# A third gate pair as block products, linear-attention scores masked by a multiply, and another order of the last transposes

## The chip, the cores and the metric

The kernel runs on one core of a Trainium2 chip, in one launch. The metric is the device time of that launch in microseconds, as the median of several runs. The engines are TensorE (PE, whose weight loads are listed apart as PEld), VectorE (DVE), ScalarE (ACT), GpSimd (POOL) and SyncE (SP), which here only issues transfers; POOL issues some too. The profile of one execution gives times from the first instruction on.

## The reference

One layer of a streaming encoder runs on 512 prompt tokens and 64 sample tokens, each with its own state:

```python
x = x + mixer(rmsnorm(x))         # gated DeltaNet branch and gated linear attention (GLA) branch
x = x + cross_attn(rmsnorm(x))    # 4 heads into 256 memory tokens
x = x + conv_ffn(rmsnorm(x))      # up, causal conv of width 3, silu gate, down
y = rmsnorm(x)
# in the mixer:
proj = h @ w_in                   # q k v b a z_a | q_b k_b v_b g_lr z_b | gt_a gt_b
o_a = rmsnorm(gated_delta(conv_silu(q, k, v), g, beta, s_a)) * silu(z_a)
o_b = rmsnorm(gla(q_b, k_b, v_b, log_a, s_b)) * silu(z_b)
merged = sigmoid(gt_a) * (o_a @ w_out_a) + sigmoid(gt_b) * (o_b @ w_out_b)
return merged @ w_o
# in gla, per chunk of 64 tokens:
a_qk = where(tri, (q * exp(G)) @ (k * exp(-G)).T, 0)
```

`x` has 1024 features. All is float32. The outputs are `y` for both streams, the new states of both recurrences and of the two convolutions, and the memory keys and values.

## The kernel before

**Layout.** Features lie on the 128 partitions in eight blocks, the 576 tokens on the free axis: 512 of the prompt, then 64 of the sample. A float32 product is made of three: weights and activations are split into a high part in a reduced format and the rest (`xh`, `xl` for the normed input, `ach`, `acl` for block sums of two operands), and high by high, high by rest and rest by high are added up in PSUM. PSUM holds four tiles called `bank` and four called `sm`.

**Plain output tiles.** A tile of 128 output features is 8 feature blocks x 3 terms x 2 column halves (256 and 320), 48 matmuls into two banks. Another engine then evacuates the two banks, and the next tile but one uses them again. The evacuation of `q`, `k`, `v` heads goes to `u` and then through the causal convolution (`c`, `th`), that of the GLA inputs to `qb`, `kb`.

**Pairs as seven products.** A pair of tiles can be made as seven products of block sums, in the manner of Winograd's variant of Strassen (P1, P2, P3 and Q4 to Q7): the 576 columns are two halves of 288, the eight feature blocks pair up to four operands, and each product has 4 x 3 = 12 matmuls of 288 columns, 84 in all. `product_order` gives their order. The weight block sums are `ws`, `sums` of raw tiles `wr`; results are added into the gate tiles `gt` (`gate_finish`). Gate tiles come in pairs (`gta`, `gtb`) for m = 0 to 7; those from `GPLAIN` on are made as products, so three pairs are plain and five products. Their activation operands, `xops`, come from a chain `c_x`, which loads `x` again (`y`) and is started in front of the tile that `XAT` names.

**Weights.** SP loads raw tiles `wr` (three buffers, `RAWB`, and one more after the pools are swapped). They become high and rest tiles `w` (six buffers, three more after the swap). In `split_summed` ACT writes minus the raw tile and its rounded form, and POOL issues a transfer that adds the raw values from memory: `w<-wt`, or `w<-ws` for a block sum. Elsewhere ACT rounds and DVE or POOL subtracts. At pair m = 5 (`GSWAP`) the buffers of the recurrences are released and their space goes to a new pool (`swap_pools`).

**What sets the order.** The order of PE is made at build time. Chains of small work, written as generators (recurrences `c_gdn`, `c_gla`, statistics `c_rstat`, gates, splits), are put between the projection matmuls where a planner thinks their inputs ready. It keeps planned times for each engine from fixed costs, places each DVE, ACT, POOL and transfer instruction at the first free planned time behind its inputs, and issues all in order of planned time. So a small edit changes the order on every engine around it, and each engine's queue runs strictly in that order. Every instruction is recorded through one helper, so that in the profile all rows have line 288.

**Statistics.** For a norm, squares of the eight blocks are added up on DVE and POOL (`acc`, `sq`), then `ssq` sums over partitions with matmuls of one column, one for each 128 tokens and each tile given to it. At the end `roots` does this with `acc` and the squares of tiles 6 and 7 (`sqt`), and POOL takes the power.

**The end.** The last block of FFN makes output tiles 6 and 7 in two column parts each, `half(m, lo, hi)`. `flip(t, i, qs)` transposes blocks of token tile t, `roots` makes its scales, `out(t)` scales (half on ACT, half on DVE) and SP stores 512 KB. Token tiles 0 and 1 need the last half; tile 4 is the sample's 64 tokens, stored in two parts `yo`.

Of the kernel before, what the change touches and what calls it, by code (L numbers as in the profile page):

```python
# [12 lines left out]
I32 = mybir.dt.int32  # L13
# [13 lines left out]
HT = T // 2  # L27
NS = 57
RAWB = 3
# [80 lines left out]
MPAIRS = [(("mo", m), ("mo", m + 1)) for m in range(2, 8, 2)]  # L110
GPLAIN = 3
GSPLIT = 6
GSWAP = 5
XAT = ("zb", 2)
GPAIRS = [(("gta", m), ("gtb", m)) for m in range(GPLAIN, 8)]
# [360 lines left out]
def tile_trunk(ctx, tc, xT, memT, wt, wd, vec, cst, w0, wgate, st_gdn, st_conv, st_gla, st_ffn, ckT, cv,  # L476
# [26 lines left out]

    def tiny(w, s="t", bufs=8):
# [419 lines left out]
    def evac(ps, t_, gap=False, o1=0, o2=TP):  # L924
        for o, i, r in zip(two(t_, gap, o1, o2), pv(ps, gap), two(N["rbc"], gap)):
            V.tensor_tensor(o, i, r, op=ALU.mult)

# [92 lines left out]
    def c_gdn(h):  # L1020
# [176 lines left out]
        if h == 4:  # L1197
# [23 lines left out]
            for i in range(4):  # L1221
                S2 = small("S", 6)
                V.scalar_tensor_tensor(S2, sgd[:, i, :], dl[:, 16 + i:17 + i], pc[:, 128 * i:128 * i + 128], op0=ALU.mult, op1=ALU.add)
                DMO(o_gdn_s[i], S2)
            yield
        S = None
        for i in range(4 if h < 4 else 0):
            ci = 4 * i + h
            if S is not None:
                pc = sm()  # L1230
                PE.matmul(pc[0:n, 0:128], ks_[i], S, start=True, stop=True)
                R = small("R", 4)[0:n, :]
# [6 lines left out]
            vn = small("vn", 4)  # L1239
# [9 lines left out]
            S2 = small("S", 6)  # L1249
# [24 lines left out]
    def c_gla(p):  # L1274
# [9 lines left out]

        def pairs(s):

            out, full = [], []
            for i in range(3):
                t_ = slot(s)
                w_ = 512 if i < 2 else 256  # L1290
                G.memset(t_[:, 0:w_], 0.0)
                yield [t_]
                v_ = t_[:, 0:w_].rearrange("p (t a b) -> p t a b", a=2, b=128)
                out += [v_[:, k] for k in range(w_ // 256)]
                full.append(v_)
            return out, full

        aqb, _ = yield from pairs("aqb")
        kgt, kgt2 = yield from pairs("kgt")
        qgp = [slot(f"qgp{j}")[:, 0:T] for j in range(2)]  # L1300
# [24 lines left out]
        for t in range(5):  # L1325
            n = 128 if t < 4 else 64
            pa = sm()
            for j in range(2):
                PE.matmul(pa[0:n, 128 * j:128 * j + n], kx[:, 128 * t:128 * t + n], qgp[j][:, 128 * t:128 * t + n], start=True, stop=True)
            V.copy_predicated(aqb[t][0:n, :, 0:n], glam[0:n, 0:n].bitcast(I32).unsqueeze(1).broadcast_to([n, 2, n]),  # L1330
                              r4(pa[0:n, 0:256])[:, :, 0:n])
            yield
        vt = []
        for j in range(2):
# [10 lines left out]
            V.tensor_tensor(r4(v1[:, 0:512]), r4(pt), N["rt"][:, 0:4].unsqueeze(2).broadcast_to([P, 4, 128]), op=ALU.mult)  # L1345
            v2 = small("vs", 4)
            V.tensor_scalar(v2[0:64, :], pt2[0:64, 0:128], N["rt"][0:64, 4:5], None, op0=ALU.mult)
# [26 lines left out]
        for j in range(2):  # L1374
            PE.matmul(pk[64 * j:64 * j + 64, 0:128], kgt[4][0:64, 0, 64 * j:64 * j + 64], vt[j][1][0:64, :], start=True, stop=True)
        S2 = small("S", 6)
        V.scalar_tensor_tensor(S2, sg_t, e1[:, T - 1:T], pk[:, 0:128], op0=ALU.mult, op1=ALU.add)
# [53 lines left out]
    def c_att(hd):  # L1431
# [42 lines left out]
        for mt_ in range(2):  # L1474
            PE.transpose(pS[:, 64 * mt_:64 * mt_ + 64], probs[2][0:64, 128 * mt_:128 * mt_ + 128], ident[0:64, 0:64])
        pst = small("pst", 2)
        A.copy(pst, pS[:, 0:128])
# [116 lines left out]
    def main():  # L1594
# [756 lines left out]
```

## Time and profile before

| | |
|---|---|
| runs | 1109.1, 1106.97, 1108.12 us, median 1108.12 |
| profiled execution | 1110.72 us, its span 1108.9 us |
| granted clock of PE, mean | 0.995 |
| busy | PE 1090.7, DVE 733.9, ACT 700.8, POOL 333.2 us |
| matmul records | 8235 |
| memory | read 160.51 MB, written 5.37 MB |

The page lists busy time by engine, then the costliest groups of instructions. A row of the timeline has its start, its length, the engine, what is written from what, the shape, how many, and in brackets how long the engine stood idle before it and for whom. In names the number of the buffer is left out. A piece of the chain of waits is given as start, length and what it was. A float32 matmul of one column or into 32 columns leaves two records.

### The profile page before, as it was taken

The numbers are of one execution on the slowest core, as the hardware profiler recorded it, in microseconds if no ns is written. First come the engines' busy times: TensorE is split into PE (matmuls) and PEld (weight loads), VectorE is DVE, ScalarE is ACT, GpSimd is POOL, SyncE is SP. The second block draws the span as 40 slices with busy tenths as digits, with TensorE's granted clock in tenths as the row PEclk, the third lists the DMA queues.
The fourth block names the chain that finished last, engine by engine and source line by source line (L and its number), as shares of the span: only waits on it lengthen the run. The fifth ranks groups of instructions, "written<-read, shape, count | busy, mean of one in ns | idle before, by whom it ended". The sixth has DMA issues, their size and how long they took to land.

```text
span 1108.9 us, 21442 instructions
## 1 busy us (share of the span) xinstructions
PE 1090.7 (98%) x8235; PEld 1050.9 (95%) x8235; DVE 733.9 (66%) x1451; ACT 700.8 (63%) x1369; POOL 333.2 (30%) x617
## 2 busy tenths in 40 slices
PE   8999999999999999999999999999999999999997
PEld 7899989998998999989999999999999999999996
DVE  6676646756564668777656667577867677677664
ACT  7566447653764687376656667855866775767553
POOL 2144114531422325131100212443432342333231
PEclk9999999999999999999999999999999999999999
DMA  8665234743564798598674729775877887788754
GB/s 270 145 152 117 59 100 83 174 98 80 142 151 93 174 216 231 173 245 195 177 203 112 190 40 215 195 170 107 180 166 171 187 203 160 171 180 177 179 111 117
DMA packets 66886, 174.88 MB, mean 158 GB/s; under 512 B 7648, under 2 KB 14176, under 8 KB 66784
## 3 DMA queue, kind: packets, MB, share of 16 engines
q0 software_dynamic: 30240, 73.41, 38.7%
q1 hardware_dynamic: 36544, 100.10, 27.6%
q8 instruction: 65, 1.06, 0.4%
q14 instruction: 37, 0.30, 0.1%
HBM read 160.51 MB, written 5.37 MB: 150 GB/s over the span
## 4 chain that ended last, share of the span: by engine, by line
PE 84%; issue 5%; ACT 3%; DMA 3%; DVE 2%; POOL 1%; SPq 0%; POOLq 0%; DVEq 0%; ACTq 0%
PE bank L288 57%; PE sm L288 27%; DMA w<-ws 2%; ACT w L288 1%; POOL w L288 1%; DMA x<-xT 1%; DMA w<-wd 0%; ACT sq L288 0%; SPq L288 0%; ACT xh L288 0%; DVE acc L288 0%; POOL acl L288 0%; DVE xl L288 0%; ACT L288 0%; DVE x L288 0%
## 5 line engine op out<-in xcount | busy, mean ns | idle before, releaser
L288 PE MATMUL bank<-xh,w 128*128 128x320 f32 (+3 forms) x1968 | 372.0, 302 | 2.7 <-DVE u L288 1.8
L288 PEld LDWEIGHTS bank<-xh,w 128*128 128x128 f32 x1968 | 299.8, 190 | 7.8 <-issue 2.8
L288 POOL DMA_DIRECT2D w<-wt x146 | 128.7, 886 | 361.4 <-ACT w L288 320.5
L288 PE MATMUL bank<-ach,w 128*128 128x320 f32 (+3 forms) x1164 | 226.3, 296 | 4.2 <-DMA w<-ws 2.3
L288 PE MATMUL bank<-xl,w 128*128 128x256 f32 (+2 forms) x984 | 219.6, 297 | 0.5 <-DVE xl L288 0.5
L288 PEld LDWEIGHTS bank<-ach,w 128*128 128x128 f32 x1164 | 183.3, 188 | 5.7 <-DMA w<-ws 3.0
L288 ACT CAST w<-wr 128x512 fp32r<-128x512 f32 (+3 forms) x200 | 158.7, 796 | 27.5 <-PE bank L288 11.3
L288 PEld LDWEIGHTS bank<-xl,w 128*128 128x128 f32 x984 | 167.8, 190 | 1.3 <-DVE xl L288 1.2
L288 ACT ACTIVATE w<-wr 128x512 fp32r<-128x512 f32 (+3 forms) x180 | 143.4, 797 | 28.2 <-PE bank L288 18.4
L288 PE MATMUL bank<-acl,w 128*128 128x256 f32 (+3 forms) x582 | 139.6, 295 | 0.3 <-DVE acl L288 0.3
L288 PE MATMUL sm<-ach,w 128*128 128x290 f32 (+1 forms) x628 | 136.0, 298 | 1.3 <-ACT w L288 0.9
L288 PEld LDWEIGHTS sm<-ach,w 128*128 128x128 f32 x628 | 104.3, 189 | 2.9 <-ACT w L288 1.1
L288 PEld LDWEIGHTS bank<-acl,w 128*128 128x128 f32 x582 | 102.6, 188 | 0.5 <-DVE acl L288 0.5
L288 ACT CAST w<-ws 128x512 fp32r<-128x512 f32 (+1 forms) x120 | 69.2, 601 | 35.2 <-DVE ws L288 20.2
L288 PE MATMUL sm<-acl,w 128*128 128x290 f32 (+1 forms) x314 | 86.5, 296 | 0.4 <-DVE acl L288 0.4
L288 DVE SCALAR_TENSOR_TENSOR fc<-fu,vec,fc 128x578 f32<-128x578 f32 x88 | 71.1, 817 | 10.5 <-ACT fc L288 10.1
L288 DVE TENSOR_TENSOR w<-ws,w 128x512 fp32r<-128x512 f32 (+1 forms) x87 | 57.7, 677 | 22.0 <-ACT w L288 19.8
L288 ACT ACTIVATE fc<-fu,vec 128x578 f32<-128x578 f32 x44 | 38.2, 870 | 35.4 <-POOL fu L288 32.5
L288 PEld LDWEIGHTS sm<-acl,w 128*128 128x128 f32 x314 | 59.2, 188 | 0.6 <-DVE acl L288 0.6
L288 DVE TENSOR_TENSOR x<-x,bank 128x256 f32<-128x256 f32 (+2 forms) x73 | 30.2, 441 | 25.4 <-PE bank L288 25.2
L288 DVE TENSOR_TENSOR ws<-ws,wr 128x512 f32<-128x512 f32 (+1 forms) x60 | 40.3, 671 | 10.2 <-DMA w<-ws 7.9
L288 PE MATMUL bank<-oh,w 128*128 128x256 f32 (+1 forms) x256 | 44.9, 295 | 0.0
(382 smaller groups left out, 1967.7 us busy)
## 6 DMA issues: line engine op xcount, KB each, us to landing
wr<-wt SPq DMA_DIRECT2D x134, 512.0 KB, 5.9
w<-wt POOLq DMA_DIRECT2D x62, 512.0 KB, 7.0
w<-wt POOLq DMA_DIRECT2D x84, 256.0 KB, 5.8
wr<-wd SPq DMA_DIRECT2D x24, 384.0 KB, 5.1
w<-wd POOLq DMA_DIRECT2D x24, 384.0 KB, 7.3
w<-ws POOLq DMA_DIRECT2D x28, 256.0 KB, 5.4
x<-xT SPq DMA_DIRECT2D x16, 288.0 KB, 4.0
y<-xT SPq DMA_DIRECT2D x8, 288.0 KB, 3.4
```

The lines of the kernel that those rows point to most:

```text
L288: fn(*args, **kw)
```

## The change

- `GPLAIN` goes from 3 to 2: the gate pair m = 2 is made as seven products too. The chain for its operands starts before `("vb", 2)` instead of `("zb", 2)`. There is one more large buffer (58), and several small rings are shorter.
- `evac` places its second and third piece as one.
- In `c_gla` the sample's scores and keys go to one small tile `g4`, so that two instead of three wide tiles are taken for each of `aqb` and `kgt` and the tiles for scores are no longer cleared. The masked scores are a product with the mask instead of a predicated copy onto zeros.
- In the first statistics the eighth square is no longer added into `acc` but given to `ssq` as a second tile.
- At the end the square of tile 6 is added into `acc` on DVE, so that `ssq` has two tiles instead of three, and `flip`, `roots` and `out` stand in another order.

```diff
-NS = 57
+NS = 58
-GPLAIN = 3
+GPLAIN = 2
-XAT = ("zb", 2)
+XAT = ("vb", 2)
...
     def evac(ps, t_, gap=False, o1=0, o2=TP):
-        for o, i, r in zip(two(t_, gap, o1, o2), pv(ps, gap), two(N["rbc"], gap)):
-            V.tensor_tensor(o, i, r, op=ALU.mult)
+        calls = [("tensor_tensor", (o, i, r), dict(op=ALU.mult)) for o, i, r in zip(two(t_, gap, o1, o2), pv(ps, gap), two(N["rbc"], gap))]
+        for c in [calls[:1], calls[1:]]:
+            V.together(c)
...
-        aqb, _ = yield from pairs("aqb")
-        kgt, kgt2 = yield from pairs("kgt")
+        g4 = small("g4", 1, 256)
+        aqs, kgs = [slot("aqb") for _ in range(2)], [slot("kgt") for _ in range(2)]
...
+        for t_ in kgs:
+            G.memset(t_[:, 0:512], 0.0)
+            yield [t_]
...
-            V.copy_predicated(aqb[t][0:n, :, 0:n], glam[0:n, 0:n].bitcast(I32).unsqueeze(1).broadcast_to([n, 2, n]),
-                              r4(pa[0:n, 0:256])[:, :, 0:n])
+            V.tensor_tensor(aqb[t][0:n, :, 0:n], r4(pa[0:n, 0:256])[:, :, 0:n], glam[0:n, 0:n].unsqueeze(1).broadcast_to([n, 2, n]), op=ALU.mult)
...
-        add(V, sqs[6], sqs[7])
+        add(V, acc, sqs[6])
         add(V, acc, sqs[4])
-        add(V, acc, sqs[6])
...
-        drv.spawn(c_rstat("n1", [(acc, 0)], 4, True, 0.0), 2)
+        drv.spawn(c_rstat("n1", [(acc, 0), (sqs[7], 0)], 4, True, 0.0), 2)
...
+            if m == 6:
+                V.tensor_tensor(acc[:, lo:hi], acc[:, lo:hi], sqt[m][:, lo:hi], op=ALU.add)
...
-                ssq([(acc, 0), (sqt[6], 0), (sqt[7], 0)], t, n, pss)
+                ssq([(acc, 0), (sqt[7], 0)], t, n, pss)
...
         half(6, 0, 256)
+        flip(2, 1, (2, 3), sm)
         roots(2, 4)
-        for t in (2, 3):
-            flip(t, 1, (2, 3), sm)
+        half(7, 0, 256)
         out(2)
-        half(7, 0, 256)
+        flip(3, 1, (2, 3), sm)
+        roots(0, 2)
         out(3)
+        for t in (0, 1):
+            flip(t, 0, range(4), sm)
+            flip(t, 1, range(4), sm)
+            out(t)
+        roots(4, 5, 64)
         for i in range(2):
             flip(4, i, range(4), bank)
-        roots(4, 5, 64)
-        roots(0, 2)
-        for t in (0, 1):
-            flip(t, 0, range(4), sm)
-        for t in (0, 1):
-            flip(t, 1, range(4), sm)
-        out(0)
-        out(1)
```

Where the order moves: first DVE, some 45 us into the program, at the evacuation of the first `v` head (`u_441`, after the change `u_443`, in three pieces) and of the first GLA query tile (`qb`); `bank_329` and after the change `bank_330` is the second bank of that `v` head. Before:

```order
L288 SCALAR_TENSOR_TENSOR c_356<-th_434,c_356 128x579
L288 TENSOR_TENSOR u_441<-bank_329,rbc_347 128x256
L288 SCALAR_TENSOR_TENSOR c_357<-u_254,vec,c_357 128x579
L288 SCALAR_TENSOR_TENSOR c_442<-u_441,vec,c_442 128x579
L288 SCALAR_TENSOR_TENSOR c_357<-th_435,c_357 128x579
L288 SCALAR_TENSOR_TENSOR qb_511<-bank_447,rbc_347 128x256
```

And with the change:

```order
L288 SCALAR_TENSOR_TENSOR c_359<-th_441,c_359 128x579
L288 SCALAR_TENSOR_TENSOR qb_513<-bank_449,rbc_350 128x256
L288 SCALAR_TENSOR_TENSOR c_360<-u_254,vec,c_360 128x579
L288 TENSOR_TENSOR u_443<-bank_330,rbc_350 128x256
L288 TENSOR_TENSOR u_443<-bank_330,rbc_350 128x64
L288 COPY sg<-sm_575 128x20
L288 SCALAR_TENSOR_TENSOR c_360<-th_442,c_360 128x579
L288 SCALAR_TENSOR_TENSOR qb_513<-bank_450,rbc_350 128x320
```

The first half of `qb` now stands where the second piece of `u` stood, and the 320 columns of its second half stand behind the copy of `sg` and a `c<-th,c`.

Then PE at the sample chain's last small matmuls (`sm<-keep,on`, the 64 sample tokens' gated DeltaNet output, which `og` on DVE reads). They stand inside the products of pair m = 4. Before:

```order
L288 MATMUL bank_4531<-xh_125,w_4512 128x288
L288 MATMUL bank_4531<-xl_126,w_4512 128x288
L288 MATMUL sm_4623<-keep,on_4581 128x64 x4
L288 MATMUL bank_4531<-xh_113,w_4512 128x288
L288 MATMUL bank_4531<-xh_117,w_4512 128x288
```

And with the change:

```order
L288 MATMUL bank_4538<-ach_3294,w_4444 128x288
L288 MATMUL bank_4538<-acl_3295,w_4444 128x288
L288 MATMUL sm_4546<-keep,on_4500 128x64 x4
L288 MATMUL bank_4538<-ach_3455,w_4444 128x288
L288 MATMUL bank_4538<-acl_3456,w_4444 128x288
```

They moved from the sixth product of that pair to its second: to the first product of pair m = 6 there were 104 matmuls, and there are 156.

Last SP's stores at the end, before:

```order
L288 DMA o_y<-wr_13576 128x1024
L288 DMA o_y<-wr_13594 128x1024
L288 DMA o_y<-yo_13647 64x512
L288 DMA o_y<-wr_13645 128x1024
L288 DMA o_y<-wr_13646 128x1024
L288 DMA o_y<-yo_13648 64x512
```

And with the change:

```order
L288 DMA o_y<-wr_13596 128x1024
L288 DMA o_y<-wr_13620 128x1024
L288 DMA o_y<-wr_13632 128x1024
L288 DMA o_y<-wr_13645 128x1024
L288 DMA o_y<-yo_13659 64x512
L288 DMA o_y<-yo_13660 64x512
```

The two stores of 64 rows are last now, behind the four of 128 rows.

More of the change, by code (lines that the diff above doesn't have):

```diff
@@ L502, in slot, with tiny @@
         return drv.rotate("s", NS, sp.tile([P, w], dt, tag="s", name=nm(s)))
-    def tiny(w, s="t", bufs=8):
+    def tiny(w, s="t", bufs=7):
         return drv.rotate(f"tiny{w}", bufs, tp.tile([P, w], F32, tag=f"tiny{w}", name=nm(s), bufs=bufs))
@@ L1221, in c_gdn @@
             for i in range(4):
-                S2 = small("S", 6)
+                S2 = small("S", 5)
                 V.scalar_tensor_tensor(S2, sgd[:, i, :], dl[:, 16 + i:17 + i], pc[:, 128 * i:128 * i + 128], op0=ALU.mult, op1=ALU.add)
@@ L1231, in c_gdn @@
                 PE.matmul(pc[0:n, 0:128], ks_[i], S, start=True, stop=True)
-                R = small("R", 4)[0:n, :]
+                R = small("R", 3)[0:n, :]
                 V.scalar_tensor_tensor(R, pc[0:n, 0:128], sg[0:n, NE, ci:ci + 1], vb[:, i, :], op0=ALU.mult, op1=ALU.add)
@@ L1238, in c_gdn @@
             PE.matmul(pc[0:n, 128:256], Y[:, i, :], R, start=True, stop=True)
-            vn = small("vn", 4)
+            vn = small("vn", 3)
             vg = small("vg", 4)
@@ L1248, in c_gdn @@
             PE.matmul(pc[0:n, 256:384], aq[:, i, :], vn[0:n, :], start=S is None, stop=True)
-            S2 = small("S", 6)
+            S2 = small("S", 5)
             if S is None:
@@ L1283, in c_gla @@
         A.activation(e3[:, 0:T], e3[:, 0:T], AF.Exp, scale=1.0 / 16)
[L1285 to L1296, printed above, removed]
-        aqb, _ = yield from pairs("aqb")
-        kgt, kgt2 = yield from pairs("kgt")
+        g4 = small("g4", 1, 256)
+        aqs, kgs = [slot("aqb") for _ in range(2)], [slot("kgt") for _ in range(2)]
+        aqb = [aqs[t // 2][:, 256 * (t % 2):256 * (t % 2) + 256].rearrange("p (a b) -> p a b", b=128) for t in range(4)]
+        aqb.append(g4[:, 0:128].rearrange("p (a b) -> p a b", b=64))
+        kgt2 = [t_[:, 0:512].rearrange("p (t a b) -> p t a b", a=2, b=128) for t_ in kgs]
+        kgt = [kgt2[t // 2][:, t % 2] for t in range(4)] + [g4[:, 128:256].unsqueeze(1)]
+        for t_ in kgs:
+            G.memset(t_[:, 0:512], 0.0)
+            yield [t_]
         qgp = [slot(f"qgp{j}")[:, 0:T] for j in range(2)]
@@ L1345, in c_gla @@
             V.tensor_tensor(r4(v1[:, 0:512]), r4(pt), N["rt"][:, 0:4].unsqueeze(2).broadcast_to([P, 4, 128]), op=ALU.mult)
-            v2 = small("vs", 4)
+            v2 = small("vs", 2)
             V.tensor_scalar(v2[0:64, :], pt2[0:64, 0:128], N["rt"][0:64, 4:5], None, op0=ALU.mult)
@@ L1375, in c_gla @@
             PE.matmul(pk[64 * j:64 * j + 64, 0:128], kgt[4][0:64, 0, 64 * j:64 * j + 64], vt[j][1][0:64, :], start=True, stop=True)
-        S2 = small("S", 6)
+        S2 = small("S", 5)
         V.scalar_tensor_tensor(S2, sg_t, e1[:, T - 1:T], pk[:, 0:128], op0=ALU.mult, op1=ALU.add)
@@ L1475, in c_att @@
             PE.transpose(pS[:, 64 * mt_:64 * mt_ + 64], probs[2][0:64, 128 * mt_:128 * mt_ + 128], ident[0:64, 0:64])
-        pst = small("pst", 2)
+        pst = small("pst", 1)
         A.copy(pst, pS[:, 0:128])
```

## Prediction

> **What bounds the kernel now.** I read the page of the profile first, then the chain that ended last, then the waits of PE. The first row is the page's busy time, the second its chain by engine; the two after them are pieces of the chain (start, length, what).
>
> ```profile
> PE 1090.7 (98%) x8235; PEld 1050.9 (95%) x8235; DVE 733.9 (66%) x1451; ACT 700.8 (63%) x1369; POOL 333.2 (30%) x617
> ...
> PE 84%; issue 5%; ACT 3%; DMA 3%; DVE 2%; POOL 1%; SPq 0%; POOLq 0%; DVEq 0%; ACTq 0%
> ...
> 63.17 18.59 PE bank L288 x140
> ...
> 495.63 3.18 PE sm L288 x24
> ```
>
> TensorE is busy for 1090.7 of 1108.9 us, and 84% of the chain is its own work. So the time is the sum of the matmuls plus the idle time of PE, some 18 us. The two pieces give the pace: plain projection matmuls (256 and 320 columns in turn) 18.59/140 = 0.1328 us each, matmuls of 288 columns 3.18/24 = 0.1325 us each. The costliest waits of PE (total, times, longest):
>
> ```profile
> PE bank L288 <- DMA w<-ws: 2.3, 3, 1.3
> PE bank L288 <- DVE u L288: 1.8, 1, 1.8
> PE bank L288 <- ACT gt L288: 1.4, 1, 1.4
> ...
> PE sm L288 <- DVE acc L288: 0.9, 1, 0.9
> ```
>
> Each is 2.3 us or less, and together they are of the size of what the edit can move. From the first output projections to the last block of FFN both kernels issue the same instructions in the same order, so differences lie in the first 430 us and in the last 15.
>
> **Part 1: the gate pair as products.** It has 96 plain matmuls now, 96 x 0.1328 = 12.75 us; as seven products it has 7 x 4 x 3 = 84 of 288 columns, 84 x 0.1325 = 11.13 us. That is **-1.6 us**, on the engine that bounds, and nothing can hide it. The four block sums of its weights and three additions of its results go to DVE (66% busy) and lie under PE as long as no buffer comes late (part 4). The operands come earlier, from a chain on ACT, DVE and SP that PE reads only at the gates: nothing.
>
> **Part 2: the first statistics.** The rows are PE's wait and its ten matmul records (five instructions), the next matmuls, and DVE's last two additions.
>
> ```profile
> 21.61 1.26 PE L288 MATMUL sm<-keep,acc 128*128 128x1 f32 x10 [0.93 <-DVE acc L288]
> 22.80 3.84 PE L288 MATMUL sm<-x,w 128*32 128x256 f32 x32
> ...
> 20.02 1.54 DVE L288 TENSOR_TENSOR acc<-acc,sq 128x576 f32<-128x576 f32 x2
> ```
>
> PE is free at 21.61 - 0.93 = 20.68. With one addition of about 0.75 fewer, and not waiting for the eighth square, the sum is there by about 20.3, so the wait goes. But the five instructions took 22.80 - 21.61 = 1.19 us, and now there are ten: 2.38 us from 20.68, ending at 23.06. **+0.2 us**: the matmuls cost what the wait gave.
>
> **Part 3: the evacuations near 46 and 54 us.** First the wait as it is, with the DVE work ahead of it.
>
> ```profile
> 45.84 0.39 PE L288 MATMUL bank<-xh,w 128*128 128x320 f32 x1 [1.78 <-DVE u L288]
> ...
> 34.79 0.26 DVE L288 COPY bt<-sm 128x32 f32<-128x32 f32 x2 [1.21 <-PE sm L288]
> ...
> 43.12 0.55 DVE L288 TENSOR_TENSOR u<-bank,rbc 128x256 f32<-128x256 f32 x2
> ...
> 44.60 0.76 DVE L288 SCALAR_TENSOR_TENSOR c<-th,c 128x579 f32<-128x579 f32 x1
> 45.27 0.42 DVE L288 TENSOR_TENSOR u<-bank,rbc 128x256 f32<-128x256 f32 x1
> ```
>
> PE waits there for the last row, the second piece of an evacuation. The change moves that piece behind its place and puts the first half of `qb` there (the order rows above): another evacuation of 256 columns, that the same PE matmul of the next tile now waits for. So the wait stays. DVE's chain from 34.79 on is released by the small gate matmuls, which now stand four projection matmuls later (4 x 0.133 = 0.53 us); the 64-column piece that left the front gives back 0.13. On that chain: 0.2 + 0.53 - 0.13 = 0.6, of which PE had 0.2 already: **+0.4 us**.
>
> Then the second half of `qb`. It stands behind the copy of `sg`, which needs two small ACT copies of a PE result, and behind a `c<-th,c` whose tanh ACT now does after them.
>
> ```profile
> 52.25 0.38 PE L288 MATMUL sm<-sg,keep 128*128 128x20 f32 x2
> ...
> 46.77 0.67 ACT L288 ACTIVATE th<-c 128x579 f32<-128x579 f32 x1
> ...
> 52.66 0.19 ACT L288 ACTIVATE sg<-sm 128x20 f32<-128x20 f32 x1 [4.28 <-PE sm L288]
> 52.74 0.18 ACT L288 ACTIVATE dl<-sm 128x20 f32<-128x20 f32 x1
> ...
> 47.63 0.76 DVE L288 SCALAR_TENSOR_TENSOR c<-th,c 128x579 f32<-128x579 f32 x1
> ...
> 53.70 0.49 DVE L288 SCALAR_TENSOR_TENSOR qb<-bank,rbc 128x320 f32<-128x320 f32 x1
> ```
>
> In the trace the half ends at 53.70 + 0.49 = 54.19, 1.6 us after the small matmuls, and twelve matmuls (1.6 us) cover it. After, ACT's two copies end 0.3 us behind the small matmuls, then tanh 0.67, `c` 0.76 and `qb` 0.49, less some overlap at their ends: 2.1 us. The small matmuls now stand four later in the pass, so only nine, 1.2 us, are left to cover it: **+0.9 us** (0.5 to 1.3), a new wait. Behind it on DVE the evacuations of `kb` are 47 matmuls (6.2 us) from being needed, after about 5.5 us of DVE work: they hold.
>
> **Part 4: the gates.** Around 380 us (DVE, SP, ACT, PE, and a piece of the chain):
>
> ```profile
> 372.86 0.86 DVE L288 SCALAR_TENSOR_TENSOR og<-sm,onh,zsamp 128x64 f32<-128x64 f32 x4 [0.40 <-PE sm L288]
> ...
> 373.92 9.75 SPq L288 DMA_DIRECT2D wr<-wt  x4
> ...
> 379.23 0.63 ACT L288 ACTIVATE w<-wr 128x512 fp32r<-128x512 f32 x1 [4.50 <-issue]
> ...
> 380.86 0.39 ACT L288 ACTIVATE gt<-bank 128x288 f32<-128x288 f32 x1
> ...
> 381.30 0.40 PE L288 MATMUL bank<-ach,w 128*128 128x288 f32 x1 [1.40 <-ACT gt L288]
> ...
> 391.11 0.93 PE L288 MATMUL bank<-ach,w 128*128 128x288 f32 x5 [0.55 <-DMA w<-ws]
> ...
> 385.01 6.06 DMA w<-ws
> ```
>
> The last user of the released pool is the sample chain's `og` at 372.86 to 373.72. SP's load into that memory issues at 373.92, ACT waits for it until 379.23, the gate evacuation is queued behind that cast until 380.86, and PE stands for 1.40 us. The casts are late from there, and the accumulating transfer issued at 385.01 lands at 391.07, another 0.6 us of PE. Before, the chain's last matmuls stand 104 matmuls ahead of pair 6's first product, after 156 (counted in the order): 52 x 0.1325 = 6.9 us more lead against a lateness of 1.4. So both should go: -2.0 us. Against it, three pairs instead of two now run before the swap, on six weight buffers and three raw ones. An accumulating transfer takes this long (median issue to landing, us):
>
> ```profile
> w<-ws POOLq DMA_DIRECT2D x28, 256.0 KB, 5.4
> ```
>
> How closely those of the first pairs land before use the waits don't tell, only that none is late now. I give one wait of half the longest seen (1.3): +0.7. Net **-1.3 us**; bounds -2.0 (nothing late) and +1.9 (the two waits stay, one full 1.3 and one 0.6 come on top).
>
> The masked scores of linear attention become a multiply in place of a predicated copy, one for one on DVE, and eight clears leave POOL (30% busy): work beside PE, worth nothing. The smaller rings may hold a chain up: -1 to +1, taken as 0.
>
> **Part 5: the end.** PE, then ACT, POOL and SP:
>
> ```profile
> 1094.72 0.28 PE L288 MATMUL bank<-keep,acc 128*128 128x1 f32 x2
> ...
> 1095.98 0.63 PE L288 MATMUL sm<-keep,gx 128*128 128x128 f32 x4
> 1096.37 0.36 PE L288 MATMUL bank<-ach,w 128*128 128x256 f32 x1
> ...
> 1097.87 1.03 PE L288 MATMUL bank<-keep,gx 128*64 128x128 f32 x8
> ...
> 1100.63 1.95 PE L288 MATMUL sm<-keep,gx 128*128 128x128 f32 x16
> ...
> 1098.52 0.42 ACT L288 ACTIVATE sq<-x 128x256 f32<-128x256 f32 x1 [0.68 <-DVE x L288]
> ...
> 1099.67 0.54 POOL L288 TENSOR_TENSOR rtf<-rin,mhalf 64x1 f32<-64x1 f32 x1 [2.55 <-DVE rin L288]
> ...
> 1104.10 0.63 SPq L288 DMA_DIRECT2D o_y<-yo  x1
> ```
>
> Six statistics matmuls take 1095.98 - 1094.72 = 1.26 us (0.21 each), four transposes 0.39. Ahead of the last half product stand four and two now: 1.04 us instead of 1.65, so it ends at 1097.26. Its square ends 1.07 us later (1098.94 - 1097.87), 1098.33; PE idles there, where eight transposes covered it. Four statistics matmuls to 1099.2, sixteen transposes (1.95) to 1101.1, the last tile's statistics to 1101.5, about 0.4 for DVE to get to them, the power 0.54, the scaling 0.75: the last output is there at 1103.2, and SP, with two issues of about 0.6, starts the last one at 1103.7, against 1104.10. **-0.4 us** (-1.2, if the small last transfer also lands sooner than one behind 512 KB rows, to +0.3).
>
> **Sum.** -1.6 + 0.2 + 0.4 + 0.9 - 1.3 - 0.4 = **-1.8 us**. The profiled execution took 1110.72 around its span of 1108.9; by it the change gives 1108.9. The median of the runs shown is 1108.12, and the forecast for the median is **1106.3 us**.
>
> **A clock that halves.** Stretches of the span; the granted clock is third from the right.
>
> ```profile
> 20.00:30.00 10.00, 9.07 (x72) 6.47 (x72) 4.21 (x11) 6.07 (x12) 5.40 (x14) 0.83 0.79 193
> ...
> 46.00:48.00 2.00, 2.00 (x12) 2.00 (x12) 1.52 (x3) 1.92 (x3) 1.27 (x2) 0.71 0.02 4
> 48.00:50.00 2.00, 2.00 (x11) 2.00 (x10) 1.45 (x3) 0.38 (x1) 0.24 (x1) 0.50 0.92 145
> ```
>
> Behind the wait of 1.78 us the clock is at one half for about 3.4 us, which costs 1.7 us; the 0.83 over 20 to 30 us is one more such stretch (0.17 x 10/0.5 = 3.4 us), behind the wait at 21 us. No such stretch follows the 1.40 us wait at 381. The Trainium skill, "TensorE: Matmul & The Clock Gate" (Part 1, and its closing table), has a free-running window of 3413 ns, and asks for no idle gaps over about 3 us. The length agrees with this trace; the 3 us do not, since 1.78 us was enough here. By the page no wait of this kernel moves the clock and the sum stands; by the trace the rivals B and D below are open.
>
> **Rivals.**
> A, slower: the pairs before the swap starve. If in each of three pairs one accumulating transfer is late by the longest seen, 1.3, and the swap's waits stay (+2.0 back), part 4 is +3.9 instead of -1.3: 1106.3 + 5.2 = 1111.5. It decides from part 4 at +2.7 on. For it: six buffers, 5.4 us to land. Against it: no wait of that kind in two such pairs now.
> B, faster: the first statistics no longer leave PE idle, the half-clock stretch behind them goes (-1.7), and no gate wait comes (-0.7): 1103.9. Against it: matmuls of one column may count as idle too.
> C, no difference: the swap's waits stay, since the loads are late for another reason (+2.0): 1108.3. That is the case in which the change does nothing but pay for its own costs.
> D: the wait at 54 us falls together with the grown one at 46 so that another stretch is halved, +1.7: 1108.0.
>
> **How the numbers follow.** Chances: forecast 0.38, A 0.14, B 0.24, C 0.16, D 0.08. A measurement of this kernel tells about 0.2%, 2.2 us, from no change: below 1105.9 is faster, above 1110.3 slower. The forecast lies close to that line: with its own range (1104.8 to 1107.8) half of it counts as faster. Faster: 0.19 + 0.23 = 0.42; slower: 0.12 from A, 0.02 from C and D; same: 0.44. The range 1103.3 to 1109.8 holds B, C, D and the forecast and leaves most of A and a little of B out.
>
> **What would show it.** After: PE's wait for `acc` gone and twenty records of one column there; the wait at 46 us named after `qb`, and a new one of about 1 us near 54 to 55; no waits at the pool swap, around 378 and 388 us; seven products for the third gate pair; the last output issued 0.4 us earlier relative to the last half product's start. Wrong would be: PE waiting for w<-ws or w<-wt in the third to fifth gate pair by more than 2 us in all, a wait of over 1.5 us in the linear attention chains, or a different number of halved stretches.

## The result, and the profile after

| | before | after |
|---|---|---|
| median of 12 runs each | 1108.13 us | 1111.08 us |
| lowest to highest | 1106.74 to 1110.70 | 1109.69 to 1113.10 |
| ratio, 95% interval | | 1.0025 [1.0016, 1.0034] |
| profiled execution, its span | 1110.72, 1108.9 us | 1109.69, 1107.1 us |

The change makes the kernel slower by about 3 us (1.8 to 3.8 by the interval). The two profiles say the opposite, 1.8 us less span, because the profiled execution of before is one of its slowest and that of after its fastest: differences between these two traces are not differences between the kernels, and the sections below use the clock and span of every run beside them.

The page of after: busy times, and the chain by engine.

```profile
PE 1087.6 (98%) x8223; PEld 1049.4 (95%) x8223; DVE 746.6 (67%) x1464; ACT 702.8 (63%) x1379; POOL 326.8 (30%) x608
...
PE 92%; DMA 2%; issue 2%; ACT 1%; DVE 1%; POOL 1%; SPq 0%; POOLq 0%; ACTq 0%
```

PE has 12 records fewer, the 96 matmuls of a pair that became 84. The ten records that the first statistics have more are those that the end has fewer (five token tiles, one matmul of two records each). PE's waits in after:

```profile
PE bank L288 <- DVE qb L288: 2.6, 2, 1.8
PE bank L288 <- DMA w<-wt: 1.7, 2, 1.1
PE bank L288 <- DMA w<-ws: 1.6, 2, 1.1
...
PE bank L288 <- DVE gt L288: 0.3, 1, 0.3
```

The wait for `u` has become one for `qb`, with a second one; the wait for `acc` is gone; at the gates the waits for `gt` and `w<-ws` have become waits for `w<-wt`. The first statistics, in the timeline of PE:

```profile
21.12 0.28 PE L288 MATMUL sm<-keep,acc 128*128 128x1 f32 x2
...
23.03 0.26 PE L288 MATMUL sm<-keep,sq 128*64 128x1 f32 x2
23.22 1.07 PE L288 MATMUL sm<-x,w 128*32 128x256 f32 x16
```

From the first to the next kind of matmul it is now 23.22 - 21.12 = 2.10 us, against 1.19 before. The two evacuations, in the timeline of PE and DVE:

```profile
44.52 0.42 DVE L288 SCALAR_TENSOR_TENSOR qb<-bank,rbc 128x256 f32<-128x256 f32 x1
...
44.99 0.63 PE L288 MATMUL bank<-xh,w 128*128 128x320 f32 x1 [1.78 <-DVE qb L288]
...
53.85 0.48 DVE L288 SCALAR_TENSOR_TENSOR qb<-bank,rbc 128x320 f32<-128x320 f32 x1
...
54.39 0.42 PE L288 MATMUL bank<-xh,w 128*128 128x320 f32 x1 [0.86 <-DVE qb L288]
```

And stretches of the span (stretch, length, PE busy, granted clock, DMA):

```profile
20.00:30.00 10.00, 10.00 (x94) 1.00 0.82 200
44.00:46.00 2.00, 1.01 (x4) 0.71 0.01 4
46.00:48.00 2.00, 2.00 (x10) 0.50 0.83 74
48.00:50.00 2.00, 2.00 (x16) 0.93 0.85 227
```

This execution has one halved stretch, behind the wait at 45 us: (0.29 + 0.50 + 0.07) x 2 = 1.7 us lost. The profiled one of before has two. So the two traces differ by 1.7 us of clock alone.

**The clock over all runs.** Each run gives a span and a mean granted clock (to 0.001, or 1.1 us, so only means over several runs say something). (1 - clock) x span is the time that the clock took; 0.4 to 2.7 us of it lie behind the last matmul in the thirteen traces, where they cost nothing. "Other" is the rest of the span. The runs of before are those made beside the experiments, on three chips; one more, of 1741 us at a mean clock of 0.56, is left out.

| kernel | runs | mean span | clock | lost to it | other |
|---|---|---|---|---|---|
| before, beside the experiments | 71 | 1106.1 | 0.9979 | 2.3 | 1103.7 |
| after | 12 | 1108.9 | 0.9963 | 4.2 | 1104.8 |

So of the 2.8 us by which the mean span grew, **1.8 are clock**, about one more halved stretch in each run, and 1.0 is other. Some of the 1.8 may lie behind the last matmul, which in the trace of after has 7.5 us behind it and in that of before 6.4. Most of it doesn't: the changed kernel with the old end, below, loses 4.3 us, where before on the same chip loses 2.7.

### The profile page after: what moved, and what is told of

The parts are those of the page before. It is cut to its first block, busy times and chain, and to the rows that moved or that the text cites. A ratio compares the mean times of both kernels' runs of the same rounds, so it can differ in the third digit from the quotient of the medians.

```text
span 1107.1 us, 21418 instructions
## 1 busy us (share of the span) xinstructions
PE 1087.6 (98%) x8223; PEld 1049.4 (95%) x8223; DVE 746.6 (67%) x1464; ACT 702.8 (63%) x1379; POOL 326.8 (30%) x608
## 4 chain that ended last, share of the span: by engine, by line
PE 92%; DMA 2%; issue 2%; ACT 1%; DVE 1%; POOL 1%; SPq 0%; POOLq 0%; ACTq 0%
PE bank L288 63%; PE sm L288 29%; DMA w<-wt 1%; ACT w L288 1%; DMA w<-ws 1%; POOL w L288 0%; DMA w<-wd 0%; DMA wr<-wt 0%; DVE xl L288 0%; ACT L288 0%; DVE acc L288 0%; ACT gna L288 0%; DVE x L288 0%; DVE c L288 0%; ACT th L288 0%
## 5 line engine op out<-in xcount | busy, mean ns | idle before, releaser
L288 PE MATMUL bank<-xh,w 128*128 128x256 f32 (+3 forms) x1928 | 366.5, 303 | 3.6 <-DVE qb L288 2.6
L288 PEld LDWEIGHTS bank<-xh,w 128*128 128x128 f32 x1928 | 294.9, 190 | 9.3 <-DVE qb L288 3.1
L288 PE MATMUL bank<-ach,w 128*128 128x288 f32 (+3 forms) x1196 | 233.0, 296 | 3.5 <-DMA w<-ws 1.6
L288 PE MATMUL bank<-xl,w 128*128 128x256 f32 (+2 forms) x964 | 216.5, 298 | 0.5 <-DVE xl L288 0.5
L288 PEld LDWEIGHTS bank<-ach,w 128*128 128x128 f32 x1196 | 188.4, 188 | 5.3 <-DMA w<-ws 2.1
L288 PEld LDWEIGHTS bank<-xl,w 128*128 128x128 f32 x964 | 164.9, 190 | 1.4 <-DVE xl L288 1.3
L288 PE MATMUL bank<-acl,w 128*128 128x256 f32 (+2 forms) x598 | 143.9, 295 | 0.3 <-DVE acl L288 0.3
L288 PEld LDWEIGHTS bank<-acl,w 128*128 128x128 f32 x598 | 105.6, 188 | 0.5 <-DVE acl L288 0.5
L288 DVE TENSOR_TENSOR w<-ws,w 128x512 fp32r<-128x512 f32 (+1 forms) x90 | 60.0, 678 | 16.6 <-ACT w L288 14.5
```

The source lines that it names most:

```text
L288: fn(*args, **kw)
```

## Experiments

Ratios are against the kernel before on the same chip, with 95% intervals.

**The end alone, and all but the end.** First the kernel before with only the new end (the square of tile 6 on DVE, two tiles for `ssq`, the new order of `flip`, `roots` and `out`):

```diff
 # before, with the last hunk of the change and:
+            if m == 6:
+                V.tensor_tensor(acc[:, lo:hi], acc[:, lo:hi], sqt[m][:, lo:hi], op=ALU.add)
-                ssq([(acc, 0), (sqt[6], 0), (sqt[7], 0)], t, n, pss)
+                ssq([(acc, 0), (sqt[7], 0)], t, n, pss)
```

> The kernel before with only the new end (order of the last transposes, roots and stores, the square of tile 6 added on DVE). Up to the last half products its order is that of before. The prediction's part 5: -0.4 us against before, because the last store issues earlier. Theory from the trace of the change (P): GpSimd closes the program with a drain of about 7.1 us from its last power on (1101.01 to 1108.16 before, 1099.20 to 1106.36 after, though SP's stores were done at 1104.22), and the new order issues that power 0.9 us later behind the last common half product: +0.9 us, with SP's stores done about 2 us ahead of the drain's end.

Then the changed kernel with the old end:

```diff
 # after, with the last hunk of the change undone:
-                ssq([(acc, 0), (sqt[7], 0)], t, n, pss)
+                ssq([(acc, 0), (sqt[6], 0), (sqt[7], 0)], t, n, pss)
```

> The changed kernel with the old end: gates, scores, rings, evacuation and first statistics as changed. The prediction without its part 5: -1.4 us against before. Theory P alone, with the rest of the measured +2.95 in the body: +2.0 us. Rival A (the gate pairs before the pool swap starve): +2 or more, with waits of PE for w<-ws and w<-wt of several us between 320 and 400 us.

Measured: 1.0006 [0.9994, 1.0019] for the end alone, and 1.0025 [1.0014, 1.0035] for all but the end (1107.76 and 1110.93 us). Without the new end the changed kernel is as slow as with it, so most of the slowdown is made in the first 430 us. What the end alone is worth the times don't resolve: the interval runs from -0.7 to +2.1 us and holds both what part 5 and what theory P expected.

**Without the third pair as products.** The same, with three plain pairs:

```diff
 # the kernel above (after with the old end), and:
-GPLAIN = 2
+GPLAIN = 3
-XAT = ("vb", 2)
+XAT = ("zb", 2)
```

> As the run before it, but with three plain gate pairs and the operand chain started where it was: what is left of the change is the first statistics, the evacuation, the scores and the rings. If the products give their 1.6 us and the loads behave: 1.6 to 2.9 us slower than the run with the third product pair. If the third product pair is what costs (rival A): about 2 us faster than that run. By the prediction's parts 2 and 3: about +1.5 us against before.

Measured: 1115.13 us, 1.0066 [1.0053, 1.0080], so 4.2 us slower than with the products, where 1.6 to 2.9 were expected. That is more than the 1.6 us that 12 matmuls make. Its clock loss is 4.8 us against 4.3. Where the rest lies isn't shown: up to the last matmul, PE stands idle for 11.6 us in the trace of this kernel and for 13.7 us in that with the products. The edit also re-times what stands around the pairs, so what the products alone are worth this pair of kernels doesn't tell.

**The last power earlier.** In after the scales of tile 4 are made last:

```diff
 # after
         flip(3, 1, (2, 3), sm)
         roots(0, 2)
+        roots(4, 5, 64)
         out(3)
...
-        roots(4, 5, 64)
         for i in range(2):
```

> The changed kernel with one call moved: the sample tile's statistics and power stand directly behind those of token tiles 0 and 1, so that GpSimd's last power is issued about 1.7 us earlier and PE does two tiny matmuls earlier. Theory P: 1.5 to 1.8 us faster than the changed kernel (about 1109.4), with the end of the span 7.8 us behind the last power or at SP's last store, whichever is later. If the last store decides (the prediction's part 5): no more than 0.3 us of difference to the changed kernel.

Measured: 1109.48 us, 1.0016 [1.0004, 1.0028], against 1.0025 for after: 1.6 us less in the median, 1.0 by the ratios, with intervals that overlap. The traces show how (end of the program, in us behind the start of the last matmul of tile 7; the closing record of POOL is in the trace beside the instructions):

| kernel | POOL's last power, start | POOL's closing record ends | SP's last issue | SP's last transfer seen landed | end of the span |
|---|---|---|---|---|---|
| before | 3.3 | 10.4 | 6.35 | 10.1 | 11.2 |
| after | 4.8 | 11.9 | 6.7 | 9.7 | 12.7 |
| power early | 3.0 | 10.1 | 6.5 | 10.1 | 11.0 |

The span ends 0.8 us behind whichever of POOL and SP is done last, and POOL is done 6.4 to 6.6 us behind the end of its last power (0.5 to 0.7 us behind the start in the table) in each of the three. After, that is what the program ends on. In the waits of SP at the end, of after:

```profile
SPq L2334 <- PEq L2334: 2.7, 2, 2.3
SPq L2334 <- DMA o_y<-yo: 1.1, 2, 0.6
```

And the last pieces of the chain, of after and of the kernel with the early power:

```profile
1097.48 1.72 issue
1099.20 0.59 POOLq L2334
1099.78 0.03 issue
1099.81 0.74 DVE yo L288
```

```profile
1099.08 0.89 PE bank L288 x8
...
1100.06 0.74 DVE yo L288
```

With the early power the last outputs hang on PE's transposes and no longer on POOL.

**The early power on the old body.** The kernel before with the new end and the early power:

```diff
 # before with the new end, and:
         roots(0, 2)
+        roots(4, 5, 64)
...
-        roots(4, 5, 64)
```

> The kernel before with the new end and the sample's power early (as in the fourth run): the body's order is that of before. Theory P: the new end is about 0.8 us slower than the old one with the late power, and 1.6 us faster than that with the early one, so about -0.8 us against before, 1107.0. If the last store decides as part 5 had it: the new end -0.4 with the power early or late.

Measured: 0.9998 [0.9987, 1.0009]: no gain. In its trace POOL is done at 10.0 us as expected, but SP's last two issues come at 6.9 and 7.5, the last transfer is seen landed at 11.4, and the span ends 12.3 us behind the same matmul. So where POOL no longer ends the program the last store can, and in these four traces it is seen landed between 9.7 and 11.4 us.

**The edits alone on the kernel before.** The evacuations (pieces two and three as one), and the linear-attention scores with the rings:

```diff
 # before, evacuations only
-        for o, i, r in zip(two(t_, gap, o1, o2), pv(ps, gap), two(N["rbc"], gap)):
-            V.tensor_tensor(o, i, r, op=ALU.mult)
+        for c in [calls[:1], calls[1:]]:
+            V.together(c)
```

> The kernel before with one edit of the change: the second and third piece of an evacuation placed as one. Its DVE order near 46 us is that of the changed kernel. Prediction's part 3: the wait near 45 us stays, now for qb, and a new one of 0.9 us comes about nine matmuls later; +0.8 us (the matmuls of the first statistics aren't moved here). The theory from the traces so far (C): beside the two waits, TensorE's clock is halved behind the first of them more often than before, since the idle time around it grows from 1.9 to about 2.3 us; a halved stretch costs 1.7 us, so +0.8 plus up to 1.5 in the median, with a mean granted clock below that of before. If neither matters: 0.

```diff
 # before, c_gla and rings only
-NS = 57
+NS = 58
-            V.copy_predicated(aqb[t][0:n, :, 0:n], ...)
+            V.tensor_tensor(aqb[t][0:n, :, 0:n], r4(pa[0:n, 0:256])[:, :, 0:n], ..., op=ALU.mult)
-                S2 = small("S", 6)
+                S2 = small("S", 5)
...
```

> The kernel before with only the edits of linear attention and of the rings (small tile for the sample, scores by a multiply, one more large buffer, shorter rings); first statistics, evacuation, gate pairs and end as before. Prediction: 0, and no more than 1 us either way. If these edits are what the body of the change loses: +2 or more, with waits in the linear attention chains between 100 and 350 us.

Measured: 1.0070 [1.0054, 1.0086] and 1.0043 [1.0029, 1.0056], 7.0 and 4.3 us slower. Each costs more alone than all edits together, and neither does what was expected of it. With the evacuations alone the wait at 45 us (1.69 us in the trace) passes at full clock, and the one behind it is 0.32 us instead of 0.9: theory C isn't seen there. Of the 7.0 and 4.3 us, 2.8 and 1.7 are clock by the runs, and in both traces a halved stretch follows a wait near 390 us, at the pool swap. The waits of PE there, evacuations only:

```profile
379.76 0.40 PE L288 MATMUL bank<-ach,w 128*128 128x288 f32 x1 [2.65 <-ACT gt L288]
...
391.24 0.93 PE L288 MATMUL bank<-ach,w 128*128 128x288 f32 x5 [2.20 <-DMA w<-ws]
...
417.17 0.80 PE L288 MATMUL bank<-oh,w 128*128 128x256 f32 x4 [2.38 <-DMA w<-wt]
```

That is 7.2 us where the trace of before has 1.40 + 0.55, and 2.75 + 1.08 stand there in the kernel with the scores and rings. A new table of planned times moves the release of the pool, the casts and the transfers behind it against PE, and these waits come out anywhere from 2 to 7 us. So the times of edits made alone cannot be added up, and the change cannot be taken apart that way.

**Old start in the changed kernel, and the new evacuations on it.**

```diff
 # after with the early power, and:
-        for c in [calls[:1], calls[1:]]:
-            V.together(c)
+        for o, i, r in zip(two(t_, gap, o1, o2), pv(ps, gap), two(N["rbc"], gap)):
+            V.tensor_tensor(o, i, r, op=ALU.mult)
-        add(V, acc, sqs[6])
+        add(V, sqs[6], sqs[7])
...
+        add(V, acc, sqs[6])
-        drv.spawn(c_rstat("n1", [(acc, 0), (sqs[7], 0)], 4, True, 0.0), 2)
+        drv.spawn(c_rstat("n1", [(acc, 0)], 4, True, 0.0), 2)
-XAT = ("vb", 2)
+XAT = ("zb", 2)
```

> The changed kernel with the first statistics and the evacuation as before, the operand chain in front of the tile where it was before, and the sample's power early at the end. If the loss lies in the start (theory C and the five extra statistics instructions, 0.9 us in the trace): the third product pair's -1.6 and the early power's -1.6 are left, about -2.5 to -3.2 us against before, 1104.6 to 1105.3. If it lies in the gates or in linear attention: no faster than before.

The second one has the evacuations of the change again (old first statistics only).

> The run before it with the changed evacuation. Prediction's part 3: 0.8 us slower than that run. Theory C: 0.8 to 2.5 us slower than it, with a lower mean granted clock. If the evacuation costs nothing: the same.

Measured: 1115.21 us, 1.0068 [1.0051, 1.0086], and 1109.67 us, 1.0017 [1.0008, 1.0027]. Both came out against what was expected: the old start isn't faster than before, and the changed evacuation made it faster and not slower. The two differ by 5.5 us, and nearly all of it is clock: lost 9.3 us against 3.0. Apart from the clock, the first is only 0.3 us below before (1103.8 against 1104.2 on its chip), so this pair says nothing for the place at 45 us. In the first the clock stays at one half in a row, around the recurrences of the sample:

```profile
320.00:330.00 10.00, 10.00 (x85) 1.00 0.34 64
330.00:335.00 5.00, 2.98 (x17) 0.74 0.00 0
335.00:340.00 5.00, 4.17 (x16) 0.50 0.00 0
340.00:345.00 5.00, 5.00 (x18) 0.50 0.00 0
345.00:350.00 5.00, 5.00 (x24) 0.56 0.57 157
```

Its waits there:

```profile
332.07 0.41 PE L288 MATMUL sm<-keep,xi 64*64 64x64 f32 x4 [1.49 <-DVE xi L288]
334.90 1.94 PE L288 MATMUL sm<-R,Y 64*64 64x128 f32 x8 [0.53 <-DVE R L288]
338.28 0.69 PE L288 MATMUL sm<-vn,aq 64*64 64x128 f32 x2 [0.82 <-ACT vn L288]
```

Three waits of 1.5 us and less, between matmuls of 64 rows: 2.8 us of waiting and some 8 us of clock ((0.26 + 0.50 + 0.50 + 0.44) x 5 = 8.5).

**Only the two evacuations of `qb`, moved.** The account by now: the loss of after is the wait for `qb` at 45 us with the halved stretch it brings, and the new wait at 54. Two DVE instructions of after (with the early power) are issued earlier; the order on PE, ACT, POOL and SP stays the same.

```diff
-                    for o, s_, r in zip(two(t_), pv(ps), two(N["rbc"])):
-                        V.scalar_tensor_tensor(o, s_, 0.125, r, op0=ALU.mult, op1=ALU.mult)
+                    for o, s_, r, e_ in zip(two(t_), pv(ps), two(N["rbc"]), (2.6, 3.2) if i == 0 else (0.0, 0.0)):
+                        V.together([("scalar_tensor_tensor", (o, s_, 0.125, r), dict(op0=ALU.mult, op1=ALU.mult))], 0.0, e_)
...
-        self.put(start, fns)
+        self.put(start - early, fns)
```

> The changed kernel with the sample's power early and two DVE instructions moved: both halves of the first qb evacuation are issued earlier (the first directly behind the first piece of the v head's, the second behind c<-th), with the order of PE, ACT, POOL and SP the same. Theory C: the waits near 45 (2.0) and 54 us (1.0) go, and with them the halved stretch at 45 us (1.7): 3.5 to 4.5 us faster than the run with the early power alone (1109.5), 1105.0 to 1106.0. If the body's loss lies elsewhere (rings, linear attention, gates): at most 3 us faster than that run with the clock as it was.

Measured: 1106.08 us, **0.9985 [0.9973, 0.9997]**, where the same kernel without the move had 1.0016 [1.0004, 1.0028]. Two instructions out of 21418 turn it from slower into faster; the gain of 3.4 us in the median is just short of the 3.5 to 4.5 expected. Its stretches:

```profile
44.00:46.00 2.00, 1.85 (x12) 1.00 0.03 8
46.00:48.00 2.00, 2.00 (x17) 1.00 0.00 0
48.00:50.00 2.00, 2.00 (x18) 1.00 0.98 147
```

PE's wait before 45 us is 0.17 us, and none is left at 54.

**One instruction on the old body.** The old body has the same place, with `u` in front. The second piece of the first `v` head's evacuation is issued right behind the first `c` rows, again with all other engines in the same order:

```diff
-            evac(ps, u, True, 3, 518)
+            for i, (o, i_, r) in enumerate(zip(two(u, True, 3, 518), pv(ps, True), two(N["rbc"], True))):
+                V.together([("tensor_tensor", (o, i_, r), dict(op=ALU.mult))], 0.0, 2.6 if col == 8 and i == 1 else 0.0)
```

> The run before it with one DVE instruction moved: the second piece of the first v head's evacuation is issued 2.6 us earlier in the planner's time, directly behind the first two, with the order of PE, ACT, POOL and SP the same. Theory C (the wait near 44 us costs its 1.8 us, and in part of the runs a stretch of half clock behind it, 1.7 us): the wait falls to 0.2 us and the mean granted clock rises: 1.6 to 2.4 us faster than the run before it, about 1104.6 to 1105.4. If PE only waits at the next place instead: the same as that run.

Measured: 1105.61 us, **0.9983 [0.9973, 0.9994]**, against 0.9998 without the move. In its trace PE is busy without a gap where before had its costliest wait:

```profile
44.00:46.00 2.00, 2.00 (x18) 1.00 0.10 14
46.00:48.00 2.00, 2.00 (x18) 1.00 0.98 152
```

Both kernels beat before and after, and both by the same place. The clock over all runs of the four:

| kernel | runs | mean span | clock | lost to it | other |
|---|---|---|---|---|---|
| after, early power | 11 | 1107.8 | 0.9964 | 4.0 | 1103.8 |
| the same, `qb` moved | 12 | 1104.0 | 0.9981 | 2.1 | 1101.9 |
| before, new end, early power | 12 | 1105.8 | 0.9978 | 2.5 | 1103.3 |
| the same, `u` moved | 12 | 1103.8 | 0.9984 | 1.8 | 1102.1 |

With `qb` moved the span is 3.8 us shorter, 1.9 of it clock and 1.9 other. The first row comes from another chip than the rest, on which before lost 2.7 us to the clock instead of 2.3: taken against before on its own chip, the gain is 3.5 us, 1.6 of it clock. With 11 and 12 runs that clock part is good to some 1.3 us; the 0.7 that `u` moved gains in clock isn't clear of the scatter. As `qb`'s two waits went together, what each is worth isn't shown.

The last and the second row settle more: with the wait taken out of both, the changed and the old body take the same time (1104.0 and 1103.8 on one chip), while with it the changed one was 1.7 us behind (each against before on its chip). So what the changed body loses, it loses at this place; apart from it, it neither gains nor loses anything that these runs resolve.

## Why the prediction was wrong

Predicted were 1106.3 us (1103.3 to 1109.8), measured 1111.08: outside the range, on the side to which I gave 0.14.

**The base.** The sum was taken against the trace of before, 1110.72 us with two halved stretches, and the forecast scaled to the median. But this execution loses 5.4 us to the clock, a mean run of before 2.3. Nor does each run have the wait for `acc`. It hangs on when the clock is first granted in full (in the trace of before two matmuls of 256 columns take 0.84 us ahead of that and 0.42 behind it), which varies by over 3 us: in the eight traces with the old statistics the wait is 0.93, 0.78 and 0.13 us where that comes at 9.3, 9.5 and 10.1 us, and there is none in the five where it comes at 10.7 to 12.1 us, since PE then reaches the statistics later. The kernel with only the new end, whose start is unchanged, is one of the five, and goes through the statistics at full clock. Its timeline of PE, and a stretch:

```profile
21.68 1.26 PE L288 MATMUL sm<-keep,acc 128*128 128x1 f32 x10
22.86 1.34 PE L288 MATMUL sm<-x,w 128*32 128x256 f32 x20
...
20.00:30.00 10.00, 10.00 (x89) 1.00 0.78 190
```

What one execution showed was treated as a cost of the kernel.

**Products, -1.6: right.** The 12 matmuls are gone from the records. Of PE's busy time 3.1 us went between the two pages, which is about these 1.6 and the 1.7 of one halved stretch less. What they gain in the run time no pair of kernels shows by itself.

**First statistics, +0.2: wrong in size.** The matmuls took 2.10 us where 2.38 were forecast, and 1.19 are replaced. But the 0.93 us that were to be won back are not there in a run without that wait: 2.10 - (22.86 - 21.68) = +0.9, by two traces. In after and in the kernel with `u` moved, whose clocks are both first granted in full at 10.7 us, the matmuls behind the statistics start at 23.22 and 22.39 us, 0.8 apart.

**Evacuations, +0.4 and +0.9: right in kind.** The wait stayed, named after `qb`, at 1.78 us as before: it did not grow by 0.4. The new one came at 54.39 us with 0.86 us.

**The clock: the step that failed.** The sum priced the wait at 45 us by its length. I had named rival D (another stretch halved, +1.7) and gave it 0.08. It is what happened: +1.8 us of clock over all runs, the largest term. The place was the 45 us wait alone rather than that one with the one at 54. In the traces, all four kernels with both new first statistics and new evacuations (and `qb` not moved) have the halved stretch near 45 us, and two of the seven kernels whose first statistics are as before (and `u` not moved); in the other five a wait of 1.67 to 1.78 us there passed at full clock. Moving two instructions took away 1.9 us of clock, give or take 1.3, and in that trace nothing is halved near 45 us: the wait for `qb` there is what brings it.

Why the changed start makes the halving regular no run was made to test, but the traces have something to say. In each of the thirteen all changes of the clock lie a whole multiple of 3.413 us apart (13.65 and 20.48 us in before, 34.13 us in after), so there is a grid of windows, and it lies differently in each execution. Idle time in the window ahead doesn't decide alone: 1.78 us was followed by a halved window three times, and passed once. How many matmuls start in it goes with it better. Take the windows at full clock, ahead of the last matmul, in which PE idled 1.0 us or more; there are 41, without one among matmuls of 64 rows. Ten were followed by a halved window, and 6 to 11 matmuls start in them; in the 31 others it is 11 to 18, where 3.413/0.1328 = 26 would fit. In the four kernels with the changed start the wait of 1.78 us has another of 0.17 us close ahead, in after

```profile
42.83 0.38 PE L288 MATMUL bank<-xh,w 128*128 128x256 f32 x1 [0.17 <-DVE u L288]
```

and their windows hold 7 to 10 matmuls; in the seven with the old statistics they hold 10 to 14. This was seen afterwards, and is no proof.

By the limit of about 3 us for a gap in the Trainium skill ("TensorE: Matmul & The Clock Gate", closing table) neither this wait of 1.78 us nor the three of up to 1.49 us in the recurrences should halve anything. The traces disagree in both places. The same page (Part 1) calls the clock's window free-running, so that it matters where in it something falls; that agrees with a wait of 1.8 us here that is followed by a halved stretch in some traces and not in others.

**Gates, -1.3: wrong.** The waits at the swap were to go (-2.0). In after:

```profile
378.46 0.93 PE L288 MATMUL bank<-ach,w 128*128 128x288 f32 x5 [1.12 <-DMA w<-wt]
...
400.38 0.40 PE L288 MATMUL bank<-ach,w 128*128 128x288 f32 x1 [0.29 <-DVE gt L288]
...
411.30 0.80 PE L288 MATMUL bank<-oh,w 128*128 128x256 f32 x4 [0.56 <-DMA w<-wt]
```

1.12 + 0.29 + 0.56 = 1.97 us, where before has 1.40 + 0.55 = 1.95. The chain's last user did come earlier (`og` at 365.78), and the wait for `gt` is gone, but the next limit is the accumulating transfer: POOL, in the timeline,

```profile
371.54 0.86 POOL L288 DMA_DIRECT2D w<-ws  x1 [4.26 <-PE bank L288]
372.58 0.85 POOL L288 DMA_DIRECT2D w<-wt  x1 [0.18 <-issue]
```

issues at 372.58 what lands at 378.4, 5.8 us later. It could not issue earlier, since the transfer ahead of it on POOL's queue had itself waited, until 371.54, in the trace last for PE. I counted the lead of the pool's release and not of POOL's transfers behind it. That is rival C, for which I gave 0.16. Rival A did not happen: in this trace no wait for `w<-ws` lies before the swap, and in two others of the same body one of 0.23 and one of 0.41 us.

**The end, -0.4: wrong in kind.** The last half product ended as forecast 0.6 us earlier, and the last store is issued 0.24 us earlier by the same landmark (that product's last matmul starts 0.62 us earlier, and the store 6.73 us behind it instead of 6.35). But the program ends on POOL, whose last power moved 1.5 us back: 1.52 - 0.62 = +0.9 us by the traces. I followed SP's last issue and did not ask which engine closes last. The times don't resolve this term (+0.06% with an interval of -0.06 to +0.19%), and the kernel with the early power on the old body didn't show the gain.

**The sum again**: -1.6 + 0.9 (first statistics) + 0 (wait at 45) + 0.9 (wait at 54) + 1.8 (clock) + 0 (swap) + 0.9 (end) = +2.9, against +2.8 in mean span and +2.95 in the median. Terms from single traces are good to some tenths each, so that the sum fits is no proof of each of them; the clock term comes from all runs, and it and the `qb` waits are the ones that an experiment showed, as one sum. There may be luck in the fit: the changed kernel with the old end, which the same sum without the end's 0.9 puts at +2.0, measured +3.2 (1.6 to 3.9).

## What to carry to other kernels

Take the time that a kernel loses to the clock from all its runs, before one trace is used as a base: here one execution lost 5.4 us to it, where a mean run loses 2.3. A wait of nearly 2 us on TensorE may cost up to twice its length, its own and that of the half clock behind it, as here in the changed body, and to move the one instruction that it waits for may be worth more than fewer matmuls. At the end of a program look for the engine that closes last, not for the last store; and where a planner re-times everything, edits made alone don't add up, so change the issue of one instruction and hold the other engines' order still.

## What was not expected of the hardware

- The clock halves for about 3.4 us also without any recorded wait. In the kernel with `qb` moved PE is busy throughout, and yet:

```profile
22.00:24.00 2.00, 2.00 (x30) 0.93 0.51 195
24.00:26.00 2.00, 2.00 (x20) 0.50 1.12 244
26.00:28.00 2.00, 2.00 (x14) 0.72 1.00 330
```

  It follows twenty records of one-column matmuls (20.82 to 22.91 us) that run in after just the same, at full clock. The kernel with three plain pairs has such a stretch too, at 24.5 us behind the same records. So small matmuls may have the effect of a wait, and not in every execution. What decides isn't shown.
- A wait of 1.49 us among small matmuls was followed by a clock of one half from about 332 to 349 us, five times 3.4 us, with two more waits of 0.53 and 0.82 us inside it.
- POOL's closing record ends 6.4 to 6.6 us behind the end of its last power, in all thirteen traces, and in the four compared above the span ends 0.8 to 0.9 us behind the last of POOL and SP.
